# A hybrid SSM and attention trunk: raw units into kept room, scan tables in order of need, a later softplus end, and an end norm with TensorE sums

## The chip, the cores and the metric

The kernel runs on one core of one Trainium2 chip. A core has TensorE (PE, matrix products, with its weight loads shown apart as PEld), VectorE (DVE), ScalarE (ACT), GpSimd (POOL) and SyncE (SP), which run side by side and wait for each other through semaphores. Each executes its own instructions strictly in the order in which the program holds them. DMAs are issued from the queues of SP, ACT and POOL and move data between HBM and the on-chip memories SBUF (128 partitions) and PSUM (where TensorE writes).

The metric is the time of one execution on the device in microseconds (us). The kernel before has a median of 1337.47 us over three runs (1337.36 to 1339.19). The profile is of one more execution, which took 1336.96 us; its span, from the first to the last instruction, is 1335.2 us, so 1.76 us of that execution lie around the span.

## The reference, cut to what matters

The trunk has two layers over 256 positions of width 2048, all in float32, and each ends in a layer norm of the residual sum.

```python
def layer_norm(x, g, b):
    mu = jnp.mean(xf, axis=-1, keepdims=True)
    var = jnp.mean(jnp.square(xf - mu), axis=-1, keepdims=True)
    return (xf - mu) * lax.rsqrt(var + LN_EPS) * g + b

def ssd_moba_mixer(x, ...):            # layer 0
    z, xbc, dt, q, k, v, gate = jnp.split(x @ w_in, SPLITS0, axis=-1)
    xbc = silu(causal_depthwise_conv(xbc, conv_w, conv_b))
    dt = softplus(dt + dt_bias)
    y_a = rms_norm((ssd_scan(xbc, dt * a) + d_skip * xh) * silu(z))
    y_b = moba_attention(rotary(q), rotary(k), v) * silu(gate)
    return concatenate([y_a, y_b]) @ w_out

def s5_mixer(x, ...):                  # layer 1
    u, gate = jnp.split(x @ w_in, 2, axis=-1)
    y = gelu(s5_ssm(u, ...))           # a diagonal complex scan in 128 groups
    ga, gb = jnp.split(y @ w_glu, 2, axis=-1)
    return (ga * sigmoid(gb) * silu(gate)) @ w_out

for layer in range(2):
    x = layer_norm(alpha * x + mixer(x), ln_g[layer], ln_b[layer])
```

## The kernel before, in words

**Weight units.** All weights stream through SBUF as units of 512 KB, in the order in which the products need them. `split_to` (L217) handles unit after unit: SP loads it into a `raw` buffer (L236, four buffers), ACT makes the rounded high part `wh` (L239), DVE the rest `wl` (L244). TensorE multiplies high by high, high by low and low by high (`xmm`, L283 and L288; L343 and L344 in the wide products, L310 in the first). A `raw` buffer is free again once its `wl` is made. Usually three units are loaded ahead. Some units are kept: their `wh` and `wl` go to tiles of their own, named `wh0` to `wh7` and so on in a pool of the stage, so that they can be used twice (`product_apart`, L392: first all of the first 128 positions, then all of the second 128).

**Around the products.** `jobs` holds work which `pump` strews between units; `back` holds work with longer leisure. `tc.issue_after` sets only where an instruction stands in the order of its engine. That order is then fixed by a scheduler before the program runs.

**The softplus of dt.** After the first products, `dt_jobs` (L508) queue `soft1` (DVE and ACT), `soft2` and `soft3` (a polynomial on POOL, L528 to L539), `soft4` (DVE: L544 and L545 take the polynomial, L548 to L552 make the cumulative decay) and `turn` (TensorE transposes at L559 and L560). The first three are queued before the x product; `soft4` and `turn` follow with the x product's first quarter, j=0 (L817). `trig_job` (L616) stands at j=1. What they make is first used by the head jobs during the z products, first at 187.2 us (L837), 77 us after L559.

**End of layer 0.** The last product of layer 0 keeps 6 units (`NKEEP`). Its rest `after0` (L1114) loads the residual rows of one half (`res0`, L1046, tile `xr`), adds them and starts the norm. `first_product` (L1137) then forms the first quarter of u while the norm is still turned into its operands (`turned`, L1096). Its eight units use `raw` buffers as all others do, four of them ahead.

**The scan of layer 1.** `u_first` (L1213) turns the first quarter of u into the tile `ut`, of which there is one buffer. `u_store` (L1210) writes it to memory from the POOL queue, and `u_load` (L1235) reads it back in another order as `um`. The wide products of the next u quarters are taken out of PSUM into `ut` too (`total`, L348 to L355). `ssm` (L1251) does sixteen blocks b: `load` brings a 896 KB table `wt` (L1258, POOL queue, four buffers), `table` (L1263) fills `rt` on POOL, `enc` (L1268) and `dec` (L1305) are small matmuls, the scan itself runs on DVE.

**The end.** The last product `product_apart(y2hl, CU, CU, after1)` (L1463) gives the first 128 rows and then, 10.9 us later (L1432 at 1313.34 and at 1324.22), the other 128. `after1` (L1440) adds the residual and takes the statistics of the last 512 columns (L1432, L1433), finishes mean and variance (`norm_stats`, L1067), and normalises in four pieces: columns 0 to 1727 in three pieces of 576 by two DVE passes each (L1455, L1456), columns 1728 to 2047 by ACT and two POOL products (L1451 to L1453). Each piece is stored by a DMA from SP or ACT (L1457). The norm's rows g and b stand in `gb1`.

Of the kernel before, what the change touches and what calls it, by code (L numbers as in the profile page):

```python
# [9 lines left out]
F32 = mybir.dt.float32  # L10
F32R = mybir.dt.float32r
# [12 lines left out]
HU = KT // HK  # L24
ALPHA = 4.0 ** 0.25
NKEEP = 6
NFIRST = 4
WARM0 = 8
WARM1 = 14
# [140 lines left out]
def trunk(tc, io, out):  # L170
# [8 lines left out]
    with ExitStack() as top:  # L179
# [33 lines left out]
        splits = {}  # L213
        keep = [None, range(0)]
        hold = [None]

        def split_to(i):  # L217
            while nsplit[0] <= min(i, len(units) - 1):
                n = nsplit[0]
                if n in early:  # L220
                    with tc.issue_after(loaded[-1].ins):
                        early.pop(n)()
                raw = st.tile([P, UK, 512], F32, tag="raw", name=nm("raw"))
                if n < 2:
                    wh = st.tile([P, UK, 512], F32R, tag="wh", name=nm("wh"))
                    wl = st.tile([P, UK, 512], F32R, tag="wl", name=nm("wl"))
                    for k in range(UK):
                        if n == 0:
                            xpart(k)
# [220 lines left out]
        with ExitStack() as l0:  # L450
# [352 lines left out]
            def xs_jobs(ps, j):  # L803
# [10 lines left out]
                while held:  # L814
                    jobs.append(held.popleft())
                held.extend([back(0), back(1)])
                jobs.extend({0: [cb_job(g) for g in range(4)] + dtj[3:], 1: [trig_job], 2: [table_job]}.get(j, []))  # L817

            for j in range(4):
                raw = sz[:, 4 * j : 4 * j + 4, :]  # L820
# [223 lines left out]
            x1 = {}  # L1044

            def res0(xr, ps, j, ts):  # L1046
                t0, t1 = ts[0], ts[-1] + 1
                nc.sync.dma_start(xr[:, t0:t1, :], io["xn"][j][:, t0:t1, :])
                for t in ts:
                    dst = x1[0][:, t, 512 * j : 512 * j + 512]  # L1050
                    V.scalar_tensor_tensor(dst, xr[:, t, :], ALPHA, ps[t], op0=OP.mult, op1=OP.add)
# [21 lines left out]
        with ExitStack() as lt:  # L1073
            tp = lt.enter_context(tc.tile_pool(name="tp", bufs=1))
            keep[0], keep[1] = tp, range(unit[0] + 2 * CU - NKEEP, unit[0] + 2 * CU)
            rows = [tp.tile([P, D], F32, name=f"row{i}") for i in range(2)]
            for i in range(2):
                nc.sync.dma_start(rows[i], lnrow(i))
# [31 lines left out]
            def step(t, i):  # L1110
                scaled(t, 4 * i, 4)
                turned(t, 4 * i, 4)

            def after0(ps, t):  # L1114
# [81 lines left out]
        with ExitStack() as l1:  # L1196
# [11 lines left out]
                return w1("ut", [P, 4, S], 1)  # L1208

            def u_store(ut, j):  # L1210
                nc.gpsimd.dma_start(ud[j].rearrange("g a c -> (g a c)").rearrange("(f p t) -> p f t", p=P, t=S), ut)

            def u_first(ps):  # L1213
                d = {}
# [16 lines left out]
                return [take, lambda: None, turn]  # L1231

            um = {}

            def u_load(hh):  # L1235
                j, h = hh // 2, hh % 2
# [14 lines left out]
            def ssm(b):  # L1251
# [3 lines left out]

                def load():
                    wt = d["w"] = w1("wt", [P, 1792], 4)
                    nc.gpsimd.dma_start(wt, wb[b])  # L1258
# [4 lines left out]
                def table():  # L1263
                    rt = d["rt"] = w1("rt", [P, 4, 64])
                    G.memset(rt[:, :, 0:1], 0.0)
                    G.tensor_copy(rt[:, :, 1:], rho[:, 4 * b : 4 * b + 4].unsqueeze(2).to_broadcast([P, 4, 63]))
# [156 lines left out]
        with ExitStack() as l2:  # L1423
            tp = l2.enter_context(tc.tile_pool(name="tp2", bufs=1))
            keep[0], keep[1] = tp, range(unit[0] + 2 * CU, unit[0] + 3 * CU)
            gb1 = big("A", [P, 4, D])
            nc.gpsimd.dma_start(gb1[:, 0, :], lnrow(2))
            nc.gpsimd.dma_start(gb1[:, 1, :], lnrow(3))

# [10 lines left out]
            def after1(ps, t):  # L1440
                def first():
                    res1(ps, 3, t)
                    norm_stats(st1, mr1, t)()
# [38 lines left out]
```

## Time and profile before

| | us |
|---|---|
| median of 3 runs | 1337.47 |
| range of the runs | 1337.36 to 1339.19 |
| the profiled execution | 1336.96 |
| its span | 1335.2 |
| mean granted TensorE clock | 0.996 |

The page of the profile lists, for each engine, the busy time within the span; a TensorE matmul counts as busy from its issue to its modelled end, and the next one starts before that, so a stall shows better as a wait, or as a late start in the timeline, than as a loss of busy time. The view of waits gives for each pair of waiting and released instruction the summed wait, the count and the longest. The timeline gives start, duration, engine, line, operation and tiles, with the idle time before it in brackets. The view of windows gives for a stretch the busy time and count of each engine, then the granted clock of TensorE, the busy share of the DMA engines, and GB/s. The chain of waits follows the work that ended last back to the start.

### The profile page before, as it was taken

Reading aid. Unit: us, or ns where it says so; the run is one execution under the profiler, and the core shown is the slowest. Engines: PE = TensorE matmul, PEld = TensorE weight load, DVE = VectorE, ACT = ScalarE, POOL = GpSimd, SP = SyncE. Lnnn points to the kernel's source line nnn. Section 1 sums busy time; section 2 is a strip of 40 time slices with the busy share of each in tenths; the row PEclk is TensorE's granted clock in tenths of the full one; section 3 lists DMA queues with packets and bytes.
Section 4 is the critical chain, followed back from the end, with each engine's and each line's share of the span. In section 5 each row is a group of like instructions: output and inputs, shape, how many; then the busy total and the mean of one; then the engine's idle time right before and its main releaser. Section 6 shows DMA issues by size and latency. Waiting matters only on the chain.

```text
span 1335.2 us, 21514 instructions
## 1 busy us (share of the span) xinstructions
PE 1318.7 (99%) x8070; PEld 1110.2 (83%) x8070; DVE 960.1 (72%) x1614; ACT 692.6 (52%) x946; POOL 343.4 (26%) x648
## 2 busy tenths in 40 slices
PE   9999999999999999999999999999999999999996
PEld 8988888877888888888888888888888888888885
DVE  6776977776686777687797766858989845555556
ACT  5566667865654554554564435444345544444441
POOL 0042000121026625334787400013454100000001
PEclk9999999999999999999999999999999999999999
DMA  8544555444556656656767778388889665555762
GB/s 321 176 176 160 187 177 172 157 158 154 178 179 224 204 204 222 213 182 206 236 192 243 251 229 319 129 327 237 300 291 332 214 217 186 187 192 187 254 216 80
DMA packets 80872, 282.72 MB, mean 212 GB/s; under 512 B 9856, under 2 KB 12544, under 8 KB 80256
## 3 DMA queue, kind: packets, MB, share of 16 engines
q1 hardware_dynamic: 68256, 239.27, 53.4%
q0 software_dynamic: 7328, 30.42, 6.8%
q10 hardware_dynamic: 5184, 11.67, 2.4%
q8 instruction: 63, 1.03, 0.3%
q14 instruction: 41, 0.34, 0.1%
HBM read 260.34 MB, written 20.97 MB: 211 GB/s over the span
## 4 chain that ended last, share of the span: by engine, by line
PE 95%; POOL 2%; DMA 2%; DVE 1%; ACT 0%; issue 0%; SPq 0%; POOLq 0%; ACTq 0%; DVEq 0%
PE main L288 60%; PE main L343 15%; PE main L344 8%; PE main L310 3%; PE aux L424 2%; DMA raw<-in_wi 1%; PE aux L867 1%; PE aux L775 1%; PE enc L1275 1%; PE dec L1320 1%; PE aux L956 1%; PE aux L988 1%; POOL ew L528 0%; PE dec L1316 0%; DMA ud<-ut 0%; PE aux L785 0%
## 5 line engine op out<-in xcount | busy, mean ns | idle before, releaser
L244 DVE TENSOR_TENSOR wl<-raw,wh 128x1024 fp32r<-128x1024 f32 x430 | 532.7, 1241 | 308.8 <-ACT wh L239 305.3
L239 ACT ACTIVATE wh<-raw 128x1024 fp32r<-128x1024 f32 x430 | 455.0, 1060 | 507.5 <-PE main L288 308.9
L288 PE MATMUL main<-wh,A 128*128 128x512 f32 x1536 | 489.9, 394 | 0.0
L288 PEld LDWEIGHTS main<-wh,A 128*128 128x128 f32 x1536 | 287.8, 188 | 59.1 <-issue 0.3
L288 PE MATMUL main<-wl,A 128*128 128x512 f32 x768 | 300.7, 392 | 0.0
L343 PE MATMUL main<-A,wh 128*128 128x512 f32 x768 | 272.9, 399 | 0.0
L288 PE MATMUL main<-wh,C 128*128 128x512 f32 x832 | 262.0, 392 | 0.3 <-ACT C L1103 0.3
L344 PE MATMUL main<-A,wl 128*128 128x256 f32 x768 | 215.3, 280 | 0.0
L288 PEld LDWEIGHTS main<-wh,C 128*128 128x128 f32 x832 | 155.6, 188 | 33.5 <-ACT C L1103 1.0
L343 PEld LDWEIGHTS main<-A,wh 128*128 128x128 f32 x768 | 144.8, 188 | 33.5
L288 PEld LDWEIGHTS main<-wl,A 128*128 128x128 f32 x768 | 144.3, 188 | 29.3 <-issue 0.5
L288 PE MATMUL main<-wl,C 128*128 128x512 f32 x416 | 162.3, 390 | 0.0
L344 PEld LDWEIGHTS main<-A,wl 128*128 128x128 f32 x768 | 145.3, 189 | 0.3
L701 POOL TENSOR_TENSOR c<-c 128x8 f32<-128x8 f32 (+2 forms) x192 | 99.8, 538 | 23.6 <-DMA wb<-c 16.0
L288 PEld LDWEIGHTS main<-wl,C 128*128 128x128 f32 x416 | 78.1, 188 | 16.1
L343 PE MATMUL main<-C,wh 128*128 128x512 f32 x192 | 68.4, 400 | 0.7 <-DVE ut L355 0.7
L876 POOL TENSOR_TENSOR ssq<-ssq,c 128x256 f32<-128x256 f32 x16 | 18.3, 1147 | 172.3 <-ACT c L874 171.8
L929 POOL TENSOR_TENSOR b<-b 128x128 f32<-128x128 f32 x16 | 11.4, 710 | 194.4 <-DVE b L928 151.6
L344 PE MATMUL main<-C,wl 128*128 128x256 f32 x192 | 53.3, 282 | 0.0
L703 POOL TENSOR_TENSOR c<-c,c 128x4 f32<-128x4 f32 (+2 forms) x96 | 48.2, 502 | 7.4
L704 POOL TENSOR_TENSOR c<-c,c 128x4 f32<-128x4 f32 (+2 forms) x96 | 45.4, 473 | 0.0
L310 PE MATMUL main<-A,wh 128*128 128x256 f32 x256 | 43.5, 284 | 1.2 <-ACT wh L231 1.2
(285 smaller groups left out, 1376.6 us busy)
## 6 DMA issues: line engine op xcount, KB each, us to landing
raw<-in_wi SPq DMA_DIRECT2D x270, 512.0 KB, 3.5
raw<-in_wo SPq DMA_DIRECT2D x96, 512.0 KB, 4.2
raw<-in_wglu SPq DMA_DIRECT2D x64, 512.0 KB, 3.4
wt<-wb POOLq DMA_DIRECT2D x16, 896.0 KB, 8.8
wb<-ob ACTq DMA_DIRECT2D x16, 512.0 KB, 5.3
bc<-in_s5bc SPq DMA_DIRECT2D x16, 256.0 KB, 3.7
wb<-c POOLq DMA_DIRECT2D x16, 256.0 KB, 3.2
wb<-om ACTq DMA_DIRECT2D x16, 128.0 KB, 3.5
```

The lines of the kernel that those rows point to most:

```text
L239: high = A.activation(wh, raw, AF.Copy)
L244: splits[n] = (loaded[-1], high, V.tensor_tensor(wl, raw, wh.bitcast(F32), op=OP.subtract))
L288: end = T.matmul(ps[o], l[:, k, sl], r[:, j, :], start=start and i == 0, stop=stop and i == 2)
L310: T.matmul(pv[o // 2][:, o % 2, :], l[:, j, sl], r[:, k, :], start=first and i == 0 and o % 2 == 0, stop=end and i == 2 and o % 2 == 1, sk ...
L343: T.matmul(ps[o], wh[:, j, sl], xx[:, k, :, :].rearrange("p a n -> p (a n)"), start=first, stop=False, skip_group_check=True)
L344: T.matmul(ps[o][:, S : 2 * S], wl[:, j, sl], xh[:, k, :], start=False, stop=end, skip_group_check=True)
L424: end = T.transpose(dst[:, i * P : i * P + P], s, ident)
L701: G.tensor_tensor(p[:, :, :, 0:m], cs[:, :, :, 1 : m + 1], cs[:, i, :, n : n + 1].unsqueeze(1).to_broadcast([P, 2, 4, m]), op=OP.mult)
L703: G.tensor_tensor(cs[:, 0, :, n + 1 : n + 1 + m], p0[:, 0, :, 0:m], p1[:, 1, :, 0:m], op=OP.subtract)
L704: G.tensor_tensor(cs[:, 1, :, n + 1 : n + 1 + m], p0[:, 1, :, 0:m], p1[:, 0, :, 0:m], op=OP.add)
L775: T.matmul(pk[at : at + 64, 64 * n + a * 16 : 64 * n + a * 16 + 16], d["ev"][:, a, 64 * i : 64 * i + 64], cv[:, a, i, :], start=True, stop ...
L876: G.tensor_tensor(ssq, ssq, jk[:, f, :], op=OP.add)
```

## The change

- **Room for raw units.** The raw data of units 4 to 7 of the first u product go to the tiles of the last layer-0 product's first four kept units (`room`), which are free once the second half of that product has used them. Units 8 to 11 thus find the four ordinary `raw` buffers earlier.
- **Softplus end.** `soft4` and `turn` move from the x product's first quarter to its second, ahead of `trig_job`.
- **Residual rows.** The last column block's residual rows are loaded for both halves in one DMA with the first half.
- **Scan tables.** On the POOL queue, tables b=1 and b=2 are to be loaded behind a u store and each later one behind the previous block's `rt`; before, four stood ahead of the first u store.
- **End norm.** For the second 128 rows, columns 0 to 895 of the residual sum are multiplied by g on DVE during the product, and TensorE copies them into PSUM with the identity matrix. Once mean and deviation are known, TensorE turns the pair into two rows, ACT copies them, and two matmuls over 2 rows add (deviation times b minus mean times g). ACT scales the sums by the reciprocal deviation and the result is stored. Columns 896 to 2047 are done by DVE in two pieces of 576. POOL no longer works on these rows; the first 128 rows are done as before.

```diff
@@ split_to
-                raw = st.tile([P, UK, 512], F32, tag="raw", name=nm("raw"))
+                if n in room:
+                    raw = keep[0].tile([P, UK, 512], F32R, tag=room[n], name=nm("raw")).bitcast(F32)
+                else:
+                    raw = st.tile([P, UK, 512], F32, tag="raw", name=nm("raw"))
@@ xs_jobs
-                jobs.extend({0: [cb_job(g) for g in range(4)] + dtj[3:], 1: [trig_job], 2: [table_job]}.get(j, []))
+                jobs.extend({0: [cb_job(g) for g in range(4)], 1: dtj[3:] + [trig_job], 2: [table_job]}.get(j, []))
@@ res0
-                t0, t1 = ts[0], ts[-1] + 1
-                nc.sync.dma_start(xr[:, t0:t1, :], io["xn"][j][:, t0:t1, :])
+                if ts[0] == 0:
+                    nc.sync.dma_start(xr, io["xn"][j])
@@ end of layer 0
+            for i in range(4):
+                room[unit[0] + 2 * CU + NFIRST + i] = f"wh{(unit[0] + 2 * CU - NKEEP + i) % 8}"
...
-                        res0(tp.tile([P, 2, 512], F32, tag="xr", name=nm("xr")), ps, 3, (t,))
+                        if not t:
+                            xlast.append(tp.tile([P, 2, 512], F32, tag="xr", name=nm("xr")))
+                        res0(xlast[0], ps, 3, (t,))
@@ u_store
+                after["u"] = nc.gpsimd.dma_start(ud[j]..., ut)
@@ ssm: load, table
-                    nc.gpsimd.dma_start(wt, wb[b])
+                    with ExitStack() as pin:
+                        if b:
+                            pin.enter_context(tc.issue_after((after[b - 1] if b > 2 else after["u"]).ins))
+                        nc.gpsimd.dma_start(wt, wb[b])
...
+                    after[b] = G.tensor_copy(rt[:, :, 1:], ...)
@@ the end (NEND = 448)
+            endp = l2.enter_context(tc.tile_pool(name="endp", bufs=1, space=PSUM))
+            sums = [endp.tile([P, 512], F32, name=f"sum{i}") for i in range(2)]
+            flip = endp.tile([2, P], F32, name="flip")
...
+            nc.sync.dma_start(gbr, io["lnr"][2:4, 0 : 2 * NEND])
+            A.activation(gbr[0:1, :], gbr[0:1, :], AF.Copy, scale=-1.0)
...
+            def last(ps):
+                mr, xv = mr1[:, 1], x1[:, 1]
+                for i in range(2):
+                    T.matmul(sums[i][:, 0:NEND], ident, xv[:, NEND * i : NEND * i + NEND], start=True, stop=False)
+                res1(ps, 3, 1)
+                V.bn_aggr(pair, st1[:, 1, :, :].rearrange("p a b -> p (a b)"))
+                V.tensor_scalar(pair[:, 1:2], pair[:, 1:2], EPS, None, op0=OP.add)
+                A.activation(pair[:, 1:2], pair[:, 1:2], AF.Sqrt)
+                T.transpose(flip, pair, ident)
+                A.activation(rowp, flip, AF.Copy)
+                for i in range(2):
+                    T.matmul(sums[i][:, 0:NEND], rowp, gbr[:, NEND * i : NEND * i + NEND], start=False, stop=True)
+                cut = [slice(2 * NEND + 576 * i, 2 * NEND + 576 * i + 576) for i in range(2)]
+                V.scalar_tensor_tensor(xv[:, cut[0]], xv[:, cut[0]], pair[:, 0:1], gb1[:, 0, cut[0]], op0=OP.subtract, op1=OP.mult)
+                V.reciprocal(mr[:, 2:3], pair[:, 1:2])
+                done = V.scalar_tensor_tensor(xv[:, cut[0]], xv[:, cut[0]], mr[:, 2:3], gb1[:, 1, cut[0]], op0=OP.mult, op1=OP.add)
+                nc.sync.dma_start(out[P:S, cut[0]], xv[:, cut[0]])
+                with tc.issue_after(done.ins):
+                    V.scalar_tensor_tensor(xv[:, cut[1]], xv[:, cut[1]], pair[:, 0:1], gb1[:, 0, cut[1]], op0=OP.subtract, op1=OP.mult)
+                V.scalar_tensor_tensor(xv[:, cut[1]], xv[:, cut[1]], mr[:, 2:3], gb1[:, 1, cut[1]], op0=OP.mult, op1=OP.add)
+                for i in range(2):
+                    sl = slice(NEND * i, NEND * i + NEND)
+                    A.activation(xv[:, sl], sums[i][:, 0:NEND], AF.Copy, scale=mr[:, 2:3])
+                    (nc.scalar if i else nc.sync).dma_start(out[P:S, sl], xv[:, sl])
+                nc.sync.dma_start(out[P:S, cut[1]], xv[:, cut[1]])
...
+                jobs.append(lambda: V.tensor_tensor(x1[:, 1, 0 : 2 * NEND], x1[:, 1, 0 : 2 * NEND], gb1[:, 0, 0 : 2 * NEND], op=OP.mult))
```

The built programs, compared engine by engine, differ in few places. TensorE's order is the same but for these: the L599 and L600 matmuls of the x product's first quarter stand 16 and 32 matmuls later, the eight transposes of its result (L424) 36 earlier, L559 and L560 91 later; the transposes of `u_first` 2 and 7 matmuls earlier, the small matmuls of the first two scan blocks up to 11 earlier; and five instructions are added at the very end. On DVE, L545 now stands behind the L355 of the next half product. On ACT, one unit's split fewer stands ahead of the second copy into `ut` (L1226), and two loads of activation tables are gone. On POOL, the order from the scan on is: table b=0, two `rt`, first u store, table b=1, eight `um` loads, second u store, table b=2, `rt`, table b=3, and so on. On SP, the residual load of the second half is gone and the small load of `gbr` is added behind the eleventh unit of the last weight. The multiply by g stands on DVE between unit splits of the last product.

More of the change, by code (lines that the diff above doesn't have):

```diff
@@ L26 @@
 NKEEP = 6
+NEND = 448
 NFIRST = 4
@@ L215, in trunk @@
         hold = [None]
+        room = {}
         def split_to(i):
@@ L1112, in step @@
                 turned(t, 4 * i, 4)
+            xlast = []
             def after0(ps, t):
@@ L1210, in u_store @@
             def u_store(ut, j):
-                nc.gpsimd.dma_start(ud[j].rearrange("g a c -> (g a c)").rearrange("(f p t) -> p f t", p=P, t=S), ut)
+                after["u"] = nc.gpsimd.dma_start(ud[j].rearrange("g a c -> (g a c)").rearrange("(f p t) -> p f t", p=P, t=S), ut)
             def u_first(ps):
@@ L1233, in trunk @@
             um = {}
+            after = {}
             def u_load(hh):
@@ L1265, in table @@
                     G.memset(rt[:, :, 0:1], 0.0)
-                    G.tensor_copy(rt[:, :, 1:], rho[:, 4 * b : 4 * b + 4].unsqueeze(2).to_broadcast([P, 4, 63]))
+                    after[b] = G.tensor_copy(rt[:, :, 1:], rho[:, 4 * b : 4 * b + 4].unsqueeze(2).to_broadcast([P, 4, 63]))
                 def enc():
@@ L1426, in trunk @@
             gb1 = big("A", [P, 4, D])
+            endp = l2.enter_context(tc.tile_pool(name="endp", bufs=1, space=PSUM))
+            sums = [endp.tile([P, 512], F32, name=f"sum{i}") for i in range(2)]
+            flip = endp.tile([2, P], F32, name="flip")
+            gbr = tp.tile([2, 2 * NEND], F32, name="gbr")
+            pair = tp.tile([P, 2], F32, name="pair")
+            rowp = tp.tile([2, P], F32, name="rowp")
+            nc.sync.dma_start(gbr, io["lnr"][2:4, 0 : 2 * NEND])
+            A.activation(gbr[0:1, :], gbr[0:1, :], AF.Copy, scale=-1.0)
             nc.gpsimd.dma_start(gb1[:, 0, :], lnrow(2))
@@ L1438, in trunk @@
                     jobs.append(lambda ps=ps, j=j, t=t: res1(ps, j, t))
+            def last(ps):
[23 more added lines that the diff above has]
+                nc.sync.dma_start(out[P:S, cut[1]], xv[:, cut[1]])
             def after1(ps, t):
+                if t:
+                    jobs.append(lambda: last(ps))
+                    return
                 def first():
```

## The prediction

> **What bounds the kernel now.** I read the page first, then TensorE's waits, then the timeline round each wait that touches a changed line, and last the end.
>
> ```profile
> span 1335.2 us, 21514 instructions
> PE 1318.7 (99%) x8070; PEld 1110.2 (83%) x8070; DVE 960.1 (72%) x1614; ACT 692.6 (52%) x946; POOL 343.4 (26%) x648
> ...
> PE 95%; POOL 2%; DMA 2%; DVE 1%; ACT 0%; issue 0%; SPq 0%; POOLq 0%; ACTq 0%; DVEq 0%
> ```
>
> TensorE is busy in 1318.7 of 1335.2 us and holds 95% of the chain that ended last. The change removes none of its matmuls; it can only win what TensorE loses by waiting, and what lies behind its last product. The page's table of TensorE's waits is short:
>
> ```profile
> PE aux L559 <- DVE ew L545: 2.1, 1, 2.1
> ...
> PE main L343 <- DVE ut L355: 0.7, 1, 0.7
> PE main L288 <- ACT C L1103: 0.3, 1, 0.3
> ```
>
> Of these, the first two belong to steps that are moved. The third (ACT's copy of a turned operand stands behind a unit's split) keeps its place in ACT's order, so I leave its 0.3 us as they are.
>
> **Softplus end.** The last step of the polynomial on POOL, the DVE instruction that takes it, and the transpose that TensorE wants:
>
> ```profile
> 108.57 0.71 POOL L539 TENSOR_TENSOR ew<-ew 32x256 f32<-32x256 f32 x1
> 109.31 0.41 DVE L545 SCALAR_TENSOR_TENSOR ew<-ew,dw 32x256 f32<-32x256 f32 x1 [5.00 <-POOL ew L539]
> 109.78 0.24 PE L559 MATMUL aux<-consts,ew 32*128 32x32 f32 x1 [2.10 <-DVE ew L545]
> ```
>
> POOL needs until 109.28. DVE sits 5.00 us in front of L545, and TensorE, in order, sits 2.10 us in front of L559. What this does to the clock shows in three windows:
>
> ```profile
> 107.20:110.60 3.40, 1.30 (x8) 0.90 (x7) 1.25 (x4) 0.00 (x0) 1.91 (x3) 1.00 0.00 0
> 110.60:114.10 3.50, 3.50 (x13) 2.69 (x12) 3.44 (x7) 2.06 (x5) 0.00 (x0) 0.51 0.30 70
> 114.10:121.00 6.90, 6.90 (x41) 5.99 (x40) 6.90 (x13) 3.98 (x6) 0.00 (x0) 1.00 0.55 190
> ```
>
> In the 3.5 us after the idle stretch TensorE got a clock of 0.51: 3.5 x 0.49 = 1.7 us are lost on top of the 2.1. The third window is normal work at 0.168 us for one matmul; the 21 records of the first two would take 21 x 0.168 = 3.5 of their 6.9 us, a loss of 3.4, and four of them are short ones of 32 columns, so the two ways agree at 3.4 to 3.8. I take 2.1 + 1.7 = 3.8.
>
> The Trainium skill, in "TensorE: Matmul & The Clock Gate", section "What's actually happening", has the clock halved after at least one idle window of about 3.4 us. Here 2.1 us of idling sufficed, so this case's trace does not agree with it; by the page's rule only the 2.1 us would be won here and the sum below would be smaller by 1.7.
>
> In the changed program L559 stands 91 matmuls later, 91 x 0.168 = 15 us, where it would be reached at about 107.7 + 15 = 123. L545 now stands on DVE behind the L355 of the next half product. That half ends on TensorE about 64 matmuls after the one shown last in its stead, 11 us on: near 115 with the stall gone; with PSUM copies, one unit's split and two short operations in front of it, 2 to 3 us by my estimate, L545 comes near 117 to 118. POOL was done at 109.3. L560 wants the scan L550, a short operation behind L545, for which I allow 1 us. So some 4 us of slack remain, and DVE does not wait at all. Ahead of the ACT copies of `turn` stands the trigonometric exponential, whose input load keeps its place on SP; the unit split behind them needs a buffer that TensorE frees only later. The eight L424 that move forward read a tile of the quarter before them, on which TensorE's list shows no wait. Term: -3.8; bounds -4.1 and, if L559 waits again as long but without halving the clock, -1.7.
>
> **Scan tables in order of need.** The second wait, in the chain and in the timeline of TensorE:
>
> ```profile
> 892.38 0.49 ACT ut L1226
> 892.87 0.28 issue
> 893.16 5.90 DMA ud<-ut
> 899.14 0.39 ACT ut L354
> 899.56 0.43 DVE ut L355
> ...
> 899.11 0.28 PE L344 MATMUL main<-C,wl 128*128 128x256 f32 x1
> 900.13 0.47 PE L343 MATMUL main<-C,wh 128*128 128x512 f32 x1 [0.74 <-DVE ut L355]
> ```
>
> There is one `ut`. Its store must land before the next quarter may be taken out of PSUM, and TensorE wants that PSUM bank: 900.13 - 899.11 instead of the usual 0.11, a loss of 0.9 us. In the changed order ACT makes the second copy into `ut` one unit's split earlier, and its transposes come 7 matmuls (7 x 0.168 = 1.2 us) earlier. With the same 5.90 us for the store, L355 ends 1.2 us earlier, which covers the 0.9. Term -0.9; bounds -1.2 (the copy wait goes too) and 0.
>
> What the new order puts in the way: on POOL's queue, table b=1 now stands behind the first u store and ahead of the eight `um` loads.
>
> ```profile
> 869.40 1.07 POOL L1258 DMA_DIRECT2D wt<-wb  x2
> 899.34 0.71 POOL L1241 DMA_DIRECT2D um<-ud  x1 [5.40 <-DMA ud<-ut]
> wt<-wb POOLq DMA_DIRECT2D x16, 896.0 KB, 8.8
> raw<-in_wi SPq DMA_DIRECT2D x270, 512.0 KB, 3.5
> ```
>
> POOL itself waits for the store (5.40 us) before it issues `um`, so table b=1 has that time to move: issued 0.8 us after the store, it has about 5 us of its median 8.8, which came from four tables behind one another and beside the weight units. About 8.8 - 5.1 = 3.7 us of a table could still be in front of `um` at worst, at best nothing. The small matmuls of block 0 stand up to 4 positions earlier and `um` is made 1.2 us earlier; I take no cost, and keep +3.7 as its end (rival 2). The later tables are issued a block ahead of their use, and four buffers remain, so I take no cost there.
>
> **Room and residual rows.** Raw units 4 to 7 now wait for TensorE to finish with the kept tiles, units 8 to 11 come earlier. In TensorE's list above no wait is on a load in this stage, and the one left there is on ACT's order. So the gain is nothing; the cover is that the split of unit 4 is wanted only after the first four units of the u product, and a load has a median of 3.5 us (`raw<-in_wi` in the fence above). If that cover failed, one load's 3.5 us would show. The residual load of 256 KB for the second half moves to the first half's, beside kept units that are loaded ahead: nothing.
>
> **The end.** The last rows, from the last product on:
>
> ```profile
> 1324.22 0.69 DVE L1432 SCALAR_TENSOR_TENSOR D<-D,main 128x512 f32<-128x512 f32 x1 [3.72 <-PE main L288]
> 1325.97 0.15 DVE L1069 TENSOR_SCALAR mr<-mr 128x1 f32<-128x1 f32 x1
> 1326.04 2.27 DVE L1455 SCALAR_TENSOR_TENSOR D<-D,mr,A 128x576 f32<-128x576 f32 x3
> 1326.16 0.20 ACT L1070 ACTIVATE mr<-mr 128x1 f32<-128x1 f32 x1 [7.77 <-DVE mr L1069]
> 1328.49 2.87 DVE L1456 SCALAR_TENSOR_TENSOR D<-D,mr,A 128x576 f32<-128x576 f32 x3
> 1329.34 1.41 POOL L1452 TENSOR_TENSOR D<-D,A 128x320 f32<-128x320 f32 x1 [8.10 <-ACT D L1451]
> 1330.83 1.25 POOL L1453 TENSOR_TENSOR D<-D,A 128x320 f32<-128x320 f32 x1
> ```
>
> Now: three first passes, then ACT, then two POOL products until 1332.08, then a store. Beside POOL the three second passes take 2.87 instead of 2.27. Prices for the new end:
>
> ```profile
> out_x<-D SPq DMA_DIRECT2D x2, 288.0 KB, 2.3
> out_x<-D ACTq DMA_DIRECT2D x4, 288.0 KB, 2.2
> out_x<-D SPq DMA_DIRECT2D x2, 160.0 KB, 2.0
> L561 ACT ACTIVATE dts<-aux x1: 196/196/196, 112.8 to 112.8; 128x64 f32<-128x64 f32 x1
> L1219 ACT ACTIVATE p<-main x2: 581/583/585, 882.7 to 883.2; 128x512 f32<-128x512 f32 x2
> ```
>
> Before: the last store is issued at 1332.1 and lands 2.0 later, 1334.1; 1.1 us of closing follow.
>
> DVE after: the same start 1326.04; four passes of 2.27 / 3 = 0.76 and a reciprocal of 0.2 end at 1329.3; SP issues there, 2.3 later it is 1331.6.
>
> ```profile
> 87.38 0.59 PE L599 MATMUL aux<-a,a 128*128 128x256 f32 x2
> 87.81 0.38 PE L600 MATMUL aux<-a,a 128*128 128x128 f32 x2
> ```
>
> TensorE and ACT after: the deviation stands at 1326.36; the transpose of the pair 0.4 by my estimate (its weights cannot be loaded ahead), ACT's copy 0.2, each with about 0.1 of handing over: 1327.2. A float32 product of 256 columns has two records here (the x2 of L599); the next matmul starts 0.43 after the first of them, so 448 columns take 0.43 x 448 / 256 = 0.75. Two of them and 0.3 of loading and draining end at 1329.0; ACT's scaling of 448 columns from PSUM is 0.583 x 448 / 512 = 0.51, to 1329.6, and its store of 224 KB lands at about 1331.8. The two identity products take 1.5 us on TensorE from 1324.2, under DVE's residual and statistics (1324.22 to 1326.12). The multiply by g, 896 columns on DVE, and the `gbr` load stand beside the last product's splits, where DVE (72% busy over the span) has gaps.
>
> 1331.8 instead of 1334.1: term -2.3. Bounds: -2.8 if the stores land after 2.0 and the handing over is free; -0.8 if the two row products and their transpose run at half clock (+1.5).
>
> **Sum.** -3.8 - 0.9 - 2.3 = -7.0. Against the profiled execution 1336.96 - 7.0 = 1330.0; that execution lies 0.5 us under the median of the runs shown, so for a median 1337.5 - 7.0 = **1330.5 us**. Its own range, all bounds on one side each: 1337.5 - 8.1 = 1329.4 to 1337.5 - 2.5 = 1335.0.
>
> **Rivals.**
> 1. The end wins little: the chain through transpose, copy, row product and scaling is four engines' handing over, none of it in the trace before. For it: each step is short work behind a semaphore. Against: the handing over shown above, L545's end at 109.72 to L559 at 109.78, took 0.06. At -0.8 the time is 1332.0, at nothing 1332.8.
> 2. `um` comes late behind table b=1. TensorE would stand in front of block 0 up to 3.7 - 1.2 = 2.5 us and then, as at L559, run 3.5 us at 0.51: +1.7. Together +4.2: 1334.7. For it: the queue's order; against: the 5.40 us that POOL waits anyway.
> The Trainium skill, in "DMA: Bandwidth & Descriptors", section "Queues, rings and completion order", says that an engine takes descriptors of one ring in ring order, which is the rule behind this rival; the trace before holds no `um` behind a table, so no row bears it out.
> 3. The softplus wait only moves: L559 waits again behind a DVE that is late by the 4 us of slack. Then -3.8 falls away: 1334.3.
> 4. Slower: rival 2 at every u quarter. From the point at which `um` is late, the second store is queued behind it and table b=2 stands before the next `um`, the single `ut` stays taken, and TensorE stands at L343 of each of the three wide quarters. If each of the three costs 3.7 of table less 1.2 and 1.7 of clock, 4.2, the sum is 1330.5 + 3 x 4.2 = 1343. It decides from a second stall on (1338.9). Against: only 0.9 us is lost at the first quarter now and no wait at the later ones is in the list, with a store and `um` loads alike there.
> 5. The change does not do what it says, all terms nothing: 1337.5. Against: the instruction orders do differ as told.
>
> **Chances.** Forecast 0.63, rival 1 0.13, rival 2 0.07, rival 3 0.05, rival 4 0.08, rival 5 0.04. A difference under 0.2%, 2.7 us, is about what a measurement of this kernel cannot tell from no change. Below 1334.8 lie the forecast and rivals 1 to 3, some of rival 2 slipping over: faster 0.86; same 0.06; slower 0.08. Range for 8 in 10: 1329.0 to 1334.8, from the forecast's lower bound, with 0.4 for the spread between runs, to rivals 2 and 3.
>
> **What would show it.** Right: no wait of TensorE at L559, no window under 1.00 near 110 and no DVE wait for POOL; no wait of L343 for L355; from the last L1432 to the last store's landing 7.6 us instead of 9.9. Wrong: a wait at an `enc` matmul for a DMA, a second stretch of half clock, ACT splits waiting for units 4 to 7, or row products over 1.0 us each. A new halving of the clock at any place costs about 1.7 us and would alone move the time by a quarter of the forecast gain.

## The result and the profile after

| | before | after |
|---|---|---|
| median of 8 executions each, us | 1337.12 | 1332.66 |
| lowest to highest, us | 1335.9 to 1343.17 | 1332.09 to 1333.44 |
| span of the profiled execution, us | 1335.2 | 1331.0 |

The ratio is 0.9958 with a 95% interval of [0.9945, 0.9972]: the changed kernel is faster by 4.5 us in the medians and by 4.2 us between the two profiled spans, where the forecast was 7.0. The executions of the changed kernel also lie within 1.4 us of each other, those before within 7.3.

Below stand the first lines of the changed kernel's page, its chain, and then rows of its view of TensorE's waits (the instruction that waited, the one that released it, us in total, times, longest). The line numbers have moved: L545 is now L550, L559 is L564, L288 is L293, L343 and L344 are L348 and L349, L1275 is L1290.

```profile
span 1331.0 us, 21530 instructions
PE 1321.8 (99%) x8079; PEld 1111.5 (84%) x8079; DVE 961.6 (72%) x1612; ACT 692.8 (52%) x947; POOL 337.9 (25%) x646
...
PE 97%; DMA 2%; DVE 0%; ACT 0%; issue 0%; SPq 0%; ACTq 0%; POOLq 0%
```

```profile
PE enc L1290 <- DVE p L1300: 0.9, 1, 0.9
PE flip L1471 <- ACT pair L1470: 0.7, 1, 0.7
PE sum L1474 <- ACT rowp L1472: 0.4, 1, 0.4
```

The softplus wait (2.1) and the `ut` wait (0.7) are gone as forecast. One wait is new and was not forecast: an encoding of the scan waits 0.9 us for DVE. The two of `flip` and `sum` belong to the new end, behind the last product.

**Softplus end.** These are the window of the stall and the one behind it, as the changed kernel runs them (busy us and count of each engine, then the granted clock), and the timeline of POOL's last step, DVE's L550 and TensorE's transposes:

```profile
104.80:108.20 3.40, 3.40 (x21) 2.94 (x20) 2.65 (x4) 2.89 (x5) 3.15 (x4) 1.00 0.49 166
108.20:111.70 3.50, 3.50 (x22) 3.03 (x21) 3.50 (x6) 2.18 (x4) 3.24 (x4) 1.00 0.32 122
```

```profile
111.97 0.73 POOL L544 TENSOR_TENSOR ew<-ew 32x256 f32<-32x256 f32 x1
...
119.37 0.40 DVE L550 SCALAR_TENSOR_TENSOR ew<-ew,dw 32x256 f32<-32x256 f32 x1
...
123.27 0.24 PE L564 MATMUL aux<-consts,ew 32*128 32x32 f32 x1
```

TensorE has no idle time there and no clock under 1.00, and the order of arrival is the one that was forecast: POOL is done at 112.7, DVE at 119.8, and TensorE wants the result at 123.3, with 3.5 us to spare at the last step.

**The new wait.** The timelines of DVE and TensorE around it:

```profile
913.14 0.41 DVE L360 TENSOR_TENSOR ut<-ut,main 128x256 f32<-128x256 f32 x1
...
913.48 1.28 DVE L1300 TENSOR_TENSOR p<-enc,wt 128x512 f32<-128x512 f32 x2
...
914.86 0.69 PE L1290 MATMUL enc<-um,wt 64*64 64x64 f32 x32 [0.92 <-DVE p L1300]
```

There is one PSUM bank `enc`. The encoding of the third block writes it, so DVE's L1300 of the second block must have read it; L1300 stands on DVE behind L360, which copies the half product that TensorE has only just finished. In the order of before, 11 product matmuls stood inside the decoding that precedes this encoding and covered it; in the new order there are none.

**Kept units.** These are the first and the last matmul of the last product's kept units in its second half, 96 steps apart, before and after:

```profile
1302.04 0.61 PE L288 MATMUL main<-wh,C 128*128 128x512 f32 x2
...
1323.80 0.39 PE L288 MATMUL main<-wh,C 128*128 128x512 f32 x1
```

```profile
1299.12 0.63 PE L293 MATMUL main<-wh,C 128*128 128x512 f32 x2
...
1321.52 0.39 PE L293 MATMUL main<-wh,C 128*128 128x512 f32 x1
```

That is 21.76 / 96 = 0.2267 us a step before and 22.40 / 96 = 0.2333 after: the same matmuls, at a full clock and without a wait, became 3% slower, 0.64 us in all.

**The end.** The rows show TensorE's row products, ACT's scaling of the two sums, and the last store:

```profile
1324.77 1.77 PE L1474 MATMUL sum<-gbr,rowp 2*128 2x448 f32 x4 [0.36 <-ACT rowp L1472]
...
1325.82 1.39 ACT L1485 ACTIVATE D<-sum,mr 128x448 f32<-128x448 f32 x2 [1.10 <-PE sum L1474]
...
1327.23 0.34 ACTq L1486 DMA_DIRECT2D out_x<-D  x1
```

From the last product's last matmul to ACT's second sum it takes 1327.21 - 1321.52 = 5.7 us; the forecast was 1329.6 - 1323.8 = 5.8. The span then ends 3.8 us after the last store's issue, where before it ended 3.1 after (1332.1 to 1335.2): this store needs 2.7 us to land instead of 2.0, and 1.0 us of closing follows in both traces. From the last product to the end of the span it takes 9.5 us instead of 11.4.

Where the 4.2 us come from shows best in the start of one and the same product matmul in both traces. The columns are its time in the trace of before; the entries are the start minus that (us), for the changed kernel and for the runs of the next section. The last two columns are the last product matmul and the span.

| kernel | 106.1 | 140.1 | 260.8 | 910.1 | 960.7 | 1300.2 | last | span |
|---|---|---|---|---|---|---|---|---|
| changed | +0.22 | -3.14 | -2.47 | -3.37 | -2.68 | -2.91 | -2.28 | -4.2 |
| e1 softplus only | +0.12 | -3.24 | -2.57 | -2.33 | -2.19 | -0.85 | -0.86 | -0.9 |
| e3 before, 8 bytes | +0.12 | +0.48 | +1.19 | +0.83 | +0.75 | +0.45 | +1.08 | +1.1 |
| e4 decoding later | -0.01 | -3.37 | -2.70 | -3.61 | -3.63 | -3.90 | -3.26 | -5.2 |
| e5 tables as before | -0.26 | -3.63 | -2.96 | -4.55 | -4.12 | -1.40 | -0.76 | -2.7 |
| e9 tables only | -0.48 | +1.31 | +2.02 | +1.10 | +1.80 | +1.54 | +1.53 | +1.5 |
| e4 and e2 together | -0.23 | -3.59 | -2.92 | -3.83 | -3.92 | -4.23 | -4.23 | -6.1 |
| and wide pairs (e10) | -0.95 | -4.59 | -4.31 | -5.80 | -6.02 | -6.24 | -6.25 | -8.2 |

For the changed kernel: a start that differs by chance +0.2, the softplus end -3.4 until 140 us, of which 0.7 comes back until 261, the scan -0.4 in sum (-0.9 by 910, +0.7 by 961, -0.2 later), the kept units +0.6, the end -1.9.

### The profile page after: what moved, and what is told of

It is laid out like the page before. It is cut to its first block, busy times and chain, and to the rows that moved or that the text cites. A ratio compares the mean times of both kernels' runs of the same rounds, so it can differ in the third digit from the quotient of the medians.

```text
span 1331.0 us, 21530 instructions
## 1 busy us (share of the span) xinstructions
PE 1321.8 (99%) x8079; PEld 1111.5 (84%) x8079; DVE 961.6 (72%) x1612; ACT 692.8 (52%) x947; POOL 337.9 (25%) x646
## 4 chain that ended last, share of the span: by engine, by line
PE 97%; DMA 2%; DVE 0%; ACT 0%; issue 0%; SPq 0%; ACTq 0%; POOLq 0%
PE main L293 61%; PE main L348 16%; PE main L349 8%; PE main L315 3%; PE aux L429 2%; DMA ud<-ut 1%; PE aux L872 1%; PE aux L780 1%; DMA um<-ud 1%; PE dec L1335 1%; PE aux L961 1%; PE enc L1290 1%; PE aux L993 1%; PE dec L1331 0%; PE aux L790 0%; PE aux L842 0%
## 5 line engine op out<-in xcount | busy, mean ns | idle before, releaser
L293 PE MATMUL main<-wh,A 128*128 128x512 f32 x1536 | 490.0, 394 | 0.0
L293 PEld LDWEIGHTS main<-wh,A 128*128 128x128 f32 x1536 | 287.8, 188 | 59.2 <-issue 0.3
L293 PE MATMUL main<-wl,A 128*128 128x512 f32 x768 | 300.7, 392 | 0.0
L348 PE MATMUL main<-A,wh 128*128 128x512 f32 x768 | 273.1, 399 | 0.0
L293 PE MATMUL main<-wh,C 128*128 128x512 f32 x832 | 262.4, 393 | 0.3 <-ACT C L1110 0.3
L349 PE MATMUL main<-A,wl 128*128 128x256 f32 x768 | 215.3, 280 | 0.0
L293 PEld LDWEIGHTS main<-wh,C 128*128 128x128 f32 x832 | 155.6, 188 | 34.0 <-ACT C L1110 1.0
L348 PEld LDWEIGHTS main<-A,wh 128*128 128x128 f32 x768 | 144.2, 188 | 33.6
L293 PEld LDWEIGHTS main<-wl,A 128*128 128x128 f32 x768 | 144.3, 188 | 29.2 <-issue 0.5
L293 PE MATMUL main<-wl,C 128*128 128x512 f32 x416 | 162.5, 391 | 0.0
L349 PEld LDWEIGHTS main<-A,wl 128*128 128x128 f32 x768 | 145.1, 189 | 0.2
L293 PEld LDWEIGHTS main<-wl,C 128*128 128x128 f32 x416 | 78.1, 188 | 16.2
L348 PE MATMUL main<-C,wh 128*128 128x512 f32 x192 | 68.2, 399 | 0.0
L934 POOL TENSOR_TENSOR b<-b 128x128 f32<-128x128 f32 x16 | 11.4, 710 | 194.5 <-DVE b L933 151.6
L349 PE MATMUL main<-C,wl 128*128 128x256 f32 x192 | 53.6, 281 | 0.0
```

What stands on the lines that cost most here:

```text
L293: end = T.matmul(ps[o], l[:, k, sl], r[:, j, :], start=start and i == 0, stop=stop and i == 2)
L348: T.matmul(ps[o], wh[:, j, sl], xx[:, k, :, :].rearrange("p a n -> p (a n)"), start=first, stop=False, skip_group_check=True)
L349: T.matmul(ps[o][:, S : 2 * S], wl[:, j, sl], xh[:, k, :], start=False, stop=end, skip_group_check=True)
```

## The experiments

**e1: the softplus end alone.** The kernel before with

```diff
-jobs.extend({0: [cb_job(g) for g in range(4)] + dtj[3:], 1: [trig_job], 2: [table_job]}.get(j, []))
+jobs.extend({0: [cb_job(g) for g in range(4)], 1: dtj[3:] + [trig_job], 2: [table_job]}.get(j, []))
```

> The kernel before with the softplus end moved to the x product's second quarter and nothing else. Theory A (the term of the prediction): the wait at the transpose and the halved clock behind it go and nothing else changes; every matmul from 120 us on starts 3.8 to 4.2 us earlier than before and the span is 1331.0 to 1331.4. Theory B (read from the changed kernel's trace): the wait and the halved clock are worth the 4.2 us, but without that stall TensorE keeps the longer rhythm of the wide products (about 0.353 us for a pair of a 512- and a 256-column matmul instead of 0.344) until about 165 us and gives 1.6 us back; from 250 us on matmuls start 2.4 to 2.8 us earlier and the span is 1332.4 to 1332.8. Median: A 1333.2, B 1334.5.

Until 261 us the run behaves as the changed kernel to 0.1 us (table): -3.4 until 140, and 0.7 comes back until 261. That is theory B in kind, with smaller sizes. At the product matmul that starts at 128.5 us before, behind all the moved ones, both runs have won 3.59 us since 106.1, not 4.2; from there to 261 us 0.9 comes back, not 1.6. What takes it back is the rhythm of the wide products. The timelines show twenty pairs of a 512- and a 256-column matmul from the first to the last row, before and then changed.

```profile
129.85 0.39 PE L343 MATMUL main<-A,wh 128*128 128x512 f32 x1
...
136.79 0.39 PE L343 MATMUL main<-A,wh 128*128 128x512 f32 x1
```

```profile
129.69 0.40 PE L348 MATMUL main<-A,wh 128*128 128x512 f32 x1
...
136.76 0.40 PE L348 MATMUL main<-A,wh 128*128 128x512 f32 x1
```

That is 6.94 / 20 = 0.347 us a pair before and 7.07 / 20 = 0.3535 after. The profiled span (1334.3) is above both theories, for a reason neither had: at 988 us TensorE waits 1.5 us for ACT's L1326 (e5 takes it up). This execution is the slowest of the five, though. The other four have spans of 1331.5 to 1332.7, and the median, 1334.41, is theory B's 1334.5. The kernel before had a median of 1340.43 in the same session, a ratio of 0.9956 [0.9944, 0.9969], which is more than theory B's gain: its executions ran from 1337.3 to 1341.9 there, and e9 shows one cause of such a spread.

**e2 and e3: where the kept tiles lie.** In e2 the changed kernel's 8-byte tile is widened; in e3 the kernel before gets such a tile.

```diff
-pair = tp.tile([P, 2], F32, name="pair")
+pair = tp.tile([P, P], F32, name="pair")[:, 0:2]
```

```diff
 gb1 = big("A", [P, 4, D])
+odd = tp.tile([P, 2], F32, name="odd")
+V.memset(odd, 0.0)
```

> The changed kernel with the 8-byte tile of the pair (mean, deviation) made 512 bytes wide, so that the kept weight tiles that are allocated behind it start on a multiple of 512 bytes again. Theory A (place in memory): the last product's kept units, which run at 0.233 us a matmul from 1299 us on in the changed kernel, return to 0.227, and the last product ends 0.6 us earlier; span 1330.4. Theory B (a rhythm that TensorE falls into whatever the addresses are): still 0.233 from 1299 us on, span 1331.0.

> The kernel before with one unused tile of 8 bytes ahead of the last product's kept weight tiles, written once and read by nobody. Theory A (place in memory): the 94 matmuls of the kept units, 0.227 us each in the kernel before, now take 0.233, and the last product ends 0.6 us later; span 1335.8. Theory B (rhythm): 0.227 as before, span 1335.2.

Theory A holds both times. These are the same 96 steps in e2 and in e3:

```profile
1299.05 0.61 PE L293 MATMUL main<-wh,C 128*128 128x512 f32 x2
...
1320.81 0.40 PE L293 MATMUL main<-wh,C 128*128 128x512 f32 x1
```

```profile
1302.49 0.39 PE L288 MATMUL main<-wh,C 128*128 128x512 f32 x1
...
1324.88 0.40 PE L288 MATMUL main<-wh,C 128*128 128x512 f32 x1
```

They take 21.76 / 96 = 0.2267 and 22.39 / 96 = 0.2332 us a step. In the program of before, the weight tiles and the activations `A`, `C` and `D` all start 32 bytes beside a multiple of 64 (not on a multiple of 512, as the first expectation has it). The 8-byte tile takes 32 bytes and puts the kept weight tiles of the last product alone on multiples of 64, while the activations `C` stay where they were. e3's span (1336.3) is larger than the 0.6 us explain; the rest is there before the kept units (+0.45 at 1300.2 in the table) and arose at and behind the stall (e9).

**e7: all operands on multiples of 64.** Together with e2's and e4's edits, 32 bytes are put ahead of the weight and activation tiles:

```diff
 pt = cst.tile([P, NPARAM], F32, name="params")
+fill = cst.tile([P, 8], F32, name="fill")
+G.memset(fill, 0.0)
```

> The changed kernel with the padded pair, the later first decoding, and one more 32-byte tile ahead of all large tiles, so that activations and weights alike start on multiples of 64 bytes instead of 32 bytes beside them. Theory A (what counts is that both operands lie alike): the matmuls stay at 0.227 us, the kept units too; span 1329.2 to 1329.5. Theory B (what counts is the place of the weights alone, and a multiple of 64 is the slow one): about 4500 matmuls of 512 columns take 0.0065 us more, most of them in products that now run at 0.227; span 1350 to 1360.

Theory A holds: the span is 1329.1, the median 1331.15, and the 96 steps take 0.2267 us each again:

```profile
1297.89 0.62 PE L295 MATMUL main<-wh,C 128*128 128x512 f32 x2
...
1319.65 0.40 PE L295 MATMUL main<-wh,C 128*128 128x512 f32 x1
```

So it is not the multiple of 64 that is slow, but weights and activations that lie differently. Weights beside a multiple of 64 with activations on one were not tried.

**e4: the third encoding later.** The first block's decoding comes one step later, and the third encoding now stands 23 product matmuls later (the expectation says 19):

```diff
-at(t + 5, act)
-at(t + 4, dec)
+at(t + 5 + (b == 0), act)
+at(t + 4 + (b == 0), dec)
```

> The changed kernel with the first scan block's decoding set one step later in the list of scan steps, which also puts the third block's encoding 19 matmuls later on TensorE. Theory A: the 0.9 us that TensorE waits at 914 us for DVE's reading of the single encoding bank goes; matmuls from 930 us on start about 1.1 us earlier than in the changed kernel, span 1329.9. Theory B: the wait only moves to the next use of that bank or to the later decoding, and the span stays at 1330.8 to 1331.2.

Theory A holds. The wait is gone and no other took its place; from 910 to 961 us the changed kernel loses 0.7, this one nothing (table). The span is 1330.0 and the median 1331.88, a ratio of 0.9936 [0.9922, 0.9949].

**e5: tables as before.** The changed kernel with `nc.gpsimd.dma_start(wt, wb[b])` unpinned again.

> The changed kernel with the scan tables loaded as before (four ahead of the first u store). Theory A: the new order of the tables is what lets the first u store run early, and what puts the encodings of the scan forward; without it TensorE waits 0.7 to 0.9 us at 897 us for the one ut tile again, and does not wait at 914 us for the encoding bank (0.9 us). The two cancel: span 1330.6 to 1331.1. Theory B: the earlier transposes of the first quarter, not the tables, remove the ut wait; then neither wait is there and the span is 1329.9 to 1330.1.

Both theories missed the span, 1332.5. The `ut` wait did not return: here too the transposes of the first quarter stand forward, within 3 matmuls of the changed kernel. So the tables are not needed to remove that wait (e5), and they are enough to remove it (e9). Of the edits that e5 keeps, the room for raw units is the one that lets ACT split earlier there; it was not tried by itself. But the run loses 2.7 us between 961 and 1010. The rows show TensorE's largest wait, ACT's timeline there, and the windows round it:

```profile
PE dec L1328 <- ACT ys L1338: 2.5, 1, 2.5
```

```profile
986.14 1.28 ACT L1338 ACT_TABLE_LOAD   x1 [4.83 <-DMA yd<-ys]
```

```profile
985.00:988.40 3.40, 0.91 (x36) 0.53 (x38) 0.00 (x0) 2.25 (x3) 0.00 (x0) 1.00 1.01 417
988.40:991.90 3.50, 3.50 (x72) 2.93 (x65) 3.07 (x5) 1.38 (x3) 0.57 (x2) 1.00 0.39 135
```

There is one tile `ys`, as there is one `ut`. Its store to `yd` must land before ACT may fill it again, TensorE's next decoding wants the bank that ACT then empties, and on the POOL queue the store stands behind two tables of 896 KB. These are the four stores of that stretch (count, KB each, median us from issue to landing) in the old order of tables, before and in e5, and in the new order, in the changed kernel:

```profile
yd<-ys POOLq DMA_DIRECT2D x4, 64.0 KB, 9.3
```

```profile
yd<-ys POOLq DMA_DIRECT2D x4, 64.0 KB, 11.2
```

```profile
yd<-ys POOLq DMA_DIRECT2D x4, 64.0 KB, 6.2
```

A 64 KB store takes 9.3 or 11.2 us behind two tables and 6.2 in the new order, where one table stands just ahead of it. In both orders the first store lands right behind the table ahead of it: at 984.7 us behind 984.2 in e5, at 978.8 behind 978.3 in the changed kernel. In the trace of before this cost TensorE only 0.3 us; it was more where TensorE came earlier (1.5 in e1, 2.5 here).

**e6: room as before.** The changed kernel without the four `room` entries.

> The changed kernel with raw units 4 to 7 of the first u product back in the four ordinary buffers; the order of the instructions on every engine stays the same. Theory A (the prediction: the step is worth nothing): TensorE has no new wait, and all its matmuls start within 0.3 us of the changed kernel's; span 1330.8 to 1331.2. Theory B: the later loads of units 8 to 11 delay ACT's splits and with them the second copy into ut; TensorE waits 0.5 to 1 us at 897 us, span 1331.5 to 1332.0.

Theory A holds: the span is 1331.1, TensorE waits for no split in that stage, and its product matmuls keep within 0.4 us of the changed kernel's.

**e8: the end as before.** The changed kernel with the old `after1` and without `last`, `endp`, `gbr` and the multiply by g.

> The changed kernel with the end of the kernel before: DVE, ACT and POOL normalise the second 128 rows, no sums on TensorE, and the kept weight tiles start where they did before. Theory A: the kept units return to 0.227 us a matmul (the last product ends 0.6 us earlier), and the time from the last matmul of that product to the end of the span goes from 9.5 back to 11.4 us; span 1331.0 - 0.6 + 1.9 = 1332.3. Theory B: the new end was worth no more than its slower kept units cost; span 1330.8 to 1331.2.

Theory A holds: the span is 1332.0, the last product's last matmul starts at 1320.56, 11.4 us before the end of the span, and the kept units run at 0.2267. The end is worth 1.9 us, and 1.3 after what its 8-byte tile cost.

**e9: the tables alone.** The kernel before with the change's edits to `u_store`, `load` and `table`.

> The kernel before with the new order of the scan tables and nothing else. Theory A: the tables' order alone moves the scan's instructions on TensorE; it removes the 0.9 us wait at 900 us for ut, brings the 0.9 to 1.1 us wait for the encoding bank some 15 us later, and removes the wait for the y store near 988 us (0.3 us in the profile before, and more in slower executions, since the store stands behind two tables of 896 KB there); span 1334.6 to 1335.1, or up to 1 us more by chance after the stall at 110 us, and a spread of the runs below 2 us, against several us for the kernel before. Theory B: the y store near 988 us has nothing to do with the tables; the spread stays, and a wait of 0.3 us or more for it is seen.

Theory A holds in its waits: there is no `ut` wait, the encoding's wait of 0.9 us is there, and none at the y store. But the profiled span, 1336.7, is beyond its range. The softplus stall is still there, and in this execution, one of the two slowest of eleven, it was much dearer than in the profile of before. These are its windows:

```profile
106.10:109.50 3.40, 1.29 (x9) 0.84 (x7) 0.67 (x2) 0.00 (x0) 2.45 (x4) 0.99 0.11 45
109.50:113.00 3.50, 3.50 (x13) 2.71 (x13) 3.43 (x8) 2.06 (x5) 0.00 (x0) 0.50 0.15 28
113.00:116.40 3.40, 3.40 (x13) 2.92 (x12) 3.37 (x8) 1.55 (x2) 0.00 (x0) 0.52 0.39 136
```

TensorE ran 6.8 us at half clock instead of 3.4, for the same idle 2.1 us. And the wide products behind it held the long rhythm here, as in e3:

```profile
129.90 0.40 PE L343 MATMUL main<-A,wh 128*128 128x512 f32 x1
...
136.97 0.40 PE L343 MATMUL main<-A,wh 128*128 128x512 f32 x1
```

That is 7.07 / 20 = 0.3535. So the price of the stall differs from one execution to the next, and of the three that were profiled with it the one of before is the cheapest: against it the same stall cost 0.4 more in e3 and 1.8 more in e9 by 140 us, and 0.7 more in each from there to 261. The spread of e9's eleven times (1335.96 to 1338.88, 2.9 us) is above the 2 us of theory A, which had put the spread on the y store, and below the 3.7 us of the kernel before in that session. e1, with the y store in its old place and no stall, spreads by 2.9 us too, so that neither of the two is shown to be the whole cause. The ratio is 0.9991 [0.9982, 1.0].

**best1: e2 and e4 together.**

> The changed kernel with the padded pair and the later first decoding together. Theory A: the two gains seen apart (0.6 us in the kept units, 0.75 us at the encoding) add up; span 1329.3 to 1329.6 and a median of 1331.2, on a chip that gives the changed kernel 1332.4. Theory B: one eats the other, span 1330.0 or more.

Theory A holds: the gains add up to a span of 1329.1 and a median of 1331.17, a ratio of 0.9945 [0.9928, 0.9963].

**e10: the wide products in pairs.** The kernel of best1 with

```diff
-for j, o in steps:
+both = [(j, o, part) for j, o in steps for part in range(2)]
+if u < HU - 1:
+    both = [(j, o, part) for j in range(HK) for part in range(2) for o in range(2)]
+for j, o, part in both:
...
-    T.matmul(ps[o], wh[:, j, sl], ...)
-    T.matmul(ps[o][:, S : 2 * S], wl[:, j, sl], ...)
+    if part == 0:
+        T.matmul(ps[o], wh[:, j, sl], ...)
+    else:
+        T.matmul(ps[o][:, S : 2 * S], wl[:, j, sl], ...)
```

> The changed kernel with padded pair and later first decoding, and in the wide products the four matmuls of a weight slice ordered 512, 512, 256, 256 columns instead of 512, 256, 512, 256. Theory A: the longer rhythm of the wide products (0.353 us for a 512- and a 256-column matmul) comes from the alternation of the two widths; with pairs it falls to 0.344 and TensorE wins up to 0.009 us a pair, 2 to 4 us between 50 and 250 us; span 1325 to 1327. Theory B: the rhythm is not set by the order of widths; span 1328.9 to 1329.3 as without the edit.

Theory A holds, at the lower end of its gain. In its timeline, sixteen pairs run from the first to the last row (x2 is two matmuls):

```profile
130.09 0.63 PE L352 MATMUL main<-A,wh 128*128 128x512 f32 x2
...
135.66 0.40 PE L352 MATMUL main<-A,wh 128*128 128x512 f32 x1
```

That is 5.57 / 16 = 0.348 us a pair, where 0.344 was expected, and by 261 us the run is 1.4 us ahead of best1. The span is 1327.0 and the median 1328.91 (1328.87 to 1329.44), a ratio of 0.9933 [0.9921, 0.9946]: this version beats both kernels.

## Why the prediction was right, and where its sum was not

The direction and the range were right, and each of the three gains is there, smaller than forecast. 1332.66 lies inside 1329.0 to 1334.8, but 2.2 us above the forecast of 1330.5; it is rival 1's number, though not by rival 1's mechanism, since the handing over at the end went as the forecast had it. Every difference from the sum goes the same way, 2.8 us in all between the profiled spans, and none cancels another; what kept the time inside the range is that the range left room for a whole term to fail.

- **Softplus, -3.8.** The mechanism is shown (e1): the wait and the halved clock go, and POOL, DVE and TensorE arrive in the order that was worked out. The size came out as -3.4 by 140 us and -2.7 by 261. The stall and the half clock alone are worth 3.6 (at the product matmul of 128.5 us), close to the 3.8. The step that failed is what the sum took for granted behind them, that both kernels then run alike. From 123.5 to about 172 us a pair of the wide products takes 0.347 in the trace before and 0.3535 in the changed one; the 33 or so pairs between 128.5 and 140 us then account for 0.0065 x 33 = 0.2, and another 0.7 goes until 261. e3 and e9, which have the stall too, held the long rhythm there, so the short one was luck of that one execution. The term was right for the stall and wrong for what one trace can stand for. Rival 3 (the wait only moves) is refuted by the waits.
- **Tables, -0.9.** The wait that was named went: 0.9 us by 910, though the tables are not the only edit that removes it (e5). The step that failed is "I take no cost" for the small matmuls: I looked at block 0 and at the loads of `um`, and the cost came from the third block's encoding, which shares one PSUM bank with the second (e4: +0.7). Rivals 2 and 4, in which `um` comes late, did not happen; no matmul waits for a load. What I did not see at all is the new order's largest effect: it takes the y store out from behind two tables. The trace before showed 0.3 us of it and I did not look into that; without the new order 1.3 us of what the softplus end wins is given back there in e1's profiled execution, its slowest, and 2.7 us in e5.
- **Room and residual rows, 0.** The term was right for the room (e6); the residual load was not tried alone, but no wait on it is seen.
- **The end, -2.3.** It measured -1.9 from the last product on (e8 confirms it). TensorE's and ACT's chain was right to 0.1 us; the last store was mis-sized: it lands 2.7 us after its issue and not 2.2, so that the sign named for the end, 7.6 us from the last residual row to the last landing, came out at 8.0. Three stores are issued within 0.8 us there; that they slow each other is possible, but was not tried.
- **Not on the list, +0.6.** The tile `pair` moved the kept weight tiles by 32 bytes (e2, e3, e7).

The sum by terms measured is +0.2 - 2.7 - 0.4 + 0.6 - 1.9 = -4.2.

## What to carry to other kernels

A wait of a few hundred nanoseconds at a single buffer can mark a place that takes back what is won ahead of it, so each such wait is followed to its store and queue before a gain upstream is counted. When instructions are put forward, every single-buffered tile between them and their neighbours is gone through, not only the one that the edit is about. A small tile in a pool can move the large ones behind it, so their addresses are compared before and after.

## What the runs showed of the hardware

- In the last product's kept units, TensorE's matmuls of 512 columns take 0.2267 us when weights and activations start alike within 64 bytes, be it both at 32 (before, e2) or both at 0 (e7), and 0.2333 when the weights start at 0 and the activations at 32 (changed, e3).
- A row of 512- and 256-column matmuls in turn runs in one of two steady rhythms, 0.347 or 0.3535 us a pair, at the same place of programs that are alike up to there (before and e9). What chooses was not found, but it is not chance alone: the nine profiled kernels without the stall and with this order of widths all hold the long one at 125 to 135 us and the short one at 185 to 195. With pairs of equal width (e10) it is 0.348.
- The clock after an idle stretch is not a matter of the stretch's length alone here. 2.1 us idle were followed by 3.4 us at half clock (before) and by 6.8 us (e9); 2.5 us idle by none (e5, both windows at 1.00). The Trainium skill, in "TensorE: Matmul & The Clock Gate", section "What's actually happening", asks for at least one idle window of about 3.4 us; the halvings after 2.1 us do not agree with that.
- The 64 KB stores on POOL's queue take 9.3 us (before) or 11.2 us (e5) to land behind two tables and 6.2 us (changed) behind one, and the first lands 0.5 us behind the table ahead of it in e5 and in the changed kernel. The Trainium skill, in "DMA: Bandwidth & Descriptors", section "Queues, rings and completion order", says of the queues of SP and ACT that an engine consumes descriptors in ring order; these landings on POOL's queue agree with such an order.
